# A product of zeros behind the gates, the norm factors and the last scores of a two-block network

## The chip, the cores and the metric

The kernel runs on one core of one Trainium2 chip, in one launch. Its time is the device time of that core in microseconds (us). Two runs took 2160.47 and 2160.67, a median of 2160.57.

## The reference, cut to what matters

The input is x, 256 tokens of 1024 float32 features. A first block mixes compressed, selected and windowed attention with a pooling mixer and adds a feed-forward layer (1024 to 4096 to 1024, squared ReLU). A second block has two layers: sliding-window attention, then a gated short convolution, each followed by an expert layer ("PEER") with 16384 experts:

```python
q = (xt @ w_query).reshape(T, PEER_HEADS, 2, QUERY_HALF)
s = jnp.einsum('thpd,hpnd->thpn', q, sub_keys)        # 8 heads x 2 x 128 scores
s_top, i_top = lax.top_k(s, PEER_TOPK)                # 16 of 128
...
g_s, sel = lax.top_k(cand, PEER_TOPK)                 # 16 of the sums
g = jax.nn.softmax(g_s, axis=-1)
...
a = jnp.einsum('td,thkd->thk', xc, u)                 # u: rows of expert_u
w = gc * jax.nn.gelu(a, approximate=False)
return jnp.einsum('thk,thkd->td', w, v)               # v: rows of expert_v
```

Everything is float32. The kernel computes the expert layer densely: all 16384 experts for all tokens, with a gate that is zero for those not chosen.

## The kernel before, in words

**Split products.** A float32 matrix is read from memory in units of 128 x 1024 (`Stream`). ScalarE rounds each unit to float32r (`wh`, line 73), VectorE or GpSimd takes what is left (`wl`, line 74). The activations are split in the same way (`xh`). `dense3` (line 179) makes three products for each 128 x 128 block: high by high, high by low, low by high, each with 256 columns (the tokens) moving. They add up in a PSUM tile, `mm`. In the profile all of them have the line of the helper `mm`, L177, and are told apart by their tiles: `mm<-xh,wh` twice, then `mm<-xh,wl`. A unit holds eight blocks, so 24 split products; two units make one pair of output tiles, 48.

**Other products on TensorE.** Some come between the split ones: `sums` (line 212, one column, the sums of squares of a norm), `spread` (line 223, float32 with the identity, which lays the norm factors along all partitions), the scores of the queries against the keys (`score`, line 1023, float32, four per pair of heads; each float32 product stands as two records in the trace), transposes, and the gates.

**An expert layer** (`peer`, line 1010). After the queries and scores comes the first half, `tmode(128, h, evac_u)`: the 128 units of `peer_u` pass through split products. Beside it run two generators, in an order that is written out by hand (`tc.manual_schedule()`): `topk` finds the chosen experts on VectorE, then `gate` spreads their gates over all experts. It works on 32 groups of eight tokens; for each group its inner function `spread` (line 1253) makes 16 half-precision products of one-hot rows (tiles `misc` and `lows`) into a PSUM tile `g2`, which ScalarE and VectorE multiply onto the experts' values (`apply`). So a gates' group of 16 half-precision products comes between every 48 (sometimes 72) split ones. The second half, `mix`, has products of 512 columns with `peer_v`.

**What sets the order.** Outside the manual part the scheduler of the tile framework places the instructions; inside it they stand as written. TensorE takes its instructions in order.

Of the kernel before, what the change touches and what calls it, by code (L numbers as in the profile page):

```python
# [8 lines left out]
F32 = mybir.dt.float32  # L9
F32R = mybir.dt.float32r  # L10
# [8 lines left out]
P = 128  # L19
# [90 lines left out]
def build(tc, a):  # L110
    nc = tc.nc
    V, S, PE, G = nc.vector, nc.scalar, nc.tensor, nc.gpsimd
    ctx = ExitStack()
    glob = ctx.enter_context(tc.tile_pool(name="glob", bufs=1))
# [32 lines left out]
    ident = glob.tile([P, P], F32, name="ident")  # L147
    V.memset(cols[:, NCOL:], 1.0)
    S.activation(cols[:, NCOL:], cols[:, NCOL:], AF.Square)
    W = Stream(nc, glob, plan, pooled)  # L150
    def load_x(k):
        nc.sync.dma_start(x[:, k:k + 2], a["x"][:, k:k + 2])

    load_x(0)
    nc.sync.dma_start(cols[:, :NCOL], a["cols"])
    W.load(0)
    load_x(2)
    W.load(1)
    load_x(4)
    W.load()  # L160
    load_x(6)
    W.load()
    nc.sync.dma_start(ident, a["consts"][:, :P])
# [8 lines left out]
    def col(name, i=0):  # L172
        o = COLS[name][0] + i
        return cols[:, o:o + 1]

    def mm(out, l, r, start, stop):
        PE.matmul(out, l, r, start=start, stop=stop, skip_group_check=True)  # L177
# [11 lines left out]
    def bank():  # L189
        return pmm.tile([P, 2, T], F32, name="mm")  # L190
# [32 lines left out]
    def spread(out, r, ps):  # L223

        for t in range(2):
            mm(ps[:, 0, t * P:(t + 1) * P], r[:, t:t + 1].to_broadcast([P, P]), ident, t == 0, True)
        V.tensor_copy(out, ps[:, 0])

    def norm_pair(i, xh, sq, gain):
# [5 lines left out]
    def square(i, sq):  # L235
        d = sq[:, :2] if i == 0 else sq[:, 2 + i % 4:4 + i % 4]
        S.activation(d, x[:, i:i + 2], AF.Square)
        if i:
            V.tensor_add(sq[:, :2], sq[:, :2], d)

    def tmode(nt, xh, evac, after=None, kt=KD, lag=0):
# [5 lines left out]
        for i in range(0, nt, 2):  # L247
            ps = bank()
            if i == 0 and lag:
                w = [W.get(), W.ahead(1)]  # L250
                for lo, hi in ((0, KD - lag), (KD - lag, KD)):
                    for j in range(2):
                        for k in range(lo, hi):
                            dense3(ps[:, j], w[j], k, xh, k, k == 0, j == 1 and k == KD - 1, j == 0)
                        if hi == KD and j == 0:
                            W.get()
                yield 0.33 * 2 * KD
# [41 lines left out]
    def con(name):  # L299
        o, w = CONSTS[name]  # L300
        return cst[:, o - P:o - P + w]
# [15 lines left out]
    for i in range(0, KD, 2):  # L317
        for k in (i, i + 1):
            parts(xh, k, x[:, k], col("mix", k))
        W.pump(i // 2 - 4)  # L320
    for i in range(0, KD, 2):
        square(i, sq)
    W.pump(-1)
    V.tensor_copy(identb, ident)
    V.tensor_copy(causalb, con("causal"))
    V.tensor_copy(bandb, con("band"))
# [41 lines left out]
    def fin_norm():  # L368
        ps = pa.tile([P, 2, T], F32, name="s", bufs=4)
        V.tensor_copy(rs2, token_rstd(sq, ps, small))  # L370
        spread(rstd, rs2, ps)
# [27 lines left out]
    ps = bank()  # L399
# [17 lines left out]
    ps = bank()  # L417
# [19 lines left out]
    ps = bank()  # L437
# [223 lines left out]
    for g in range(0, 4, 2):  # L661
        ps = bank()
        for j in range(2):
            dense3(ps[:, j], (h, l), g + j, ph, g + j, True, j == 1, j == 0)
        for j in range(2):
            parts(mh, g + j, ps[:, j], col("pscale", g + j))
# [42 lines left out]
    for _ in tmode(8, ah, residual(0.5, lambda k: col("mlp", k), xh, sq), lag=2):  # L709
        pass  # L710
# [21 lines left out]
    def after_ff(i):  # L732
        if i == 0:
            ps = pf.tile([P, 2, T], F32, name="s")
            r = token_rstd(sq, ps, small)
            V.tensor_mul(r, r, r)
            spread(rstd2, r, ps)
# [221 lines left out]
    for _ in tmode(4, xh, evac_q, after_qk):  # L959
        pass  # L960
    spread(rstd2, r1s[0], pa.tile([P, 2, T], F32, name="s", bufs=3))
    late_q(2)
    turn_k()
    query_scale(0)
    ps = bank()
# [41 lines left out]
    def side_bank():  # L1007
        return px.tile([P, 2, T], F32, name="g", bufs=2)

    def peer(l, xg, sq, rest):  # L1010
# [12 lines left out]
        def score(i):  # L1023
            ps = side_bank()
            q = qs[(i // 2) % 3]
            for t in range(2):
                for p in range(2):
                    mm(ps[:, t, p * P:(p + 1) * P], q[:, p, t * P:(t + 1) * P], keys[:, i + p],
                       t == 0 and p == 0, True)
            S.copy(sc4[:, i // 2].rearrange("p t h k -> p (t h k)"), ps.rearrange("p a b -> p (a b)"))  # L1030

        def evac_q(i, ps):
            if i < 6:
                S.copy(qs[i // 2], ps)
                if i == 2:
                    hm.append(token_rstd(sq, side_bank(), small))
                if i == 4:
                    spread(rstd, hm.pop(), side_bank())
                    for q in qs:
                        V.tensor_mul(q, q, bc(rstd, 2))  # L1040
            else:
                score(i - 6)
                V.tensor_mul(qs[(i // 2) % 3], ps, bc(rstd, 2))
# [14 lines left out]
        V.scalar_tensor_tensor(t, x[:, k], col("ffn2", 8 * l + k), rstd, op0=OP.mult, op1=OP.mult)  # L1058
        parts(h, k, t)
        score(10)  # L1060
        score(12)
        score(14)
        gA2 = xhp.tile([P, 16, T], F32, name="xh1")
# [162 lines left out]
        def gate():  # L1226

            m = glob.tile([P, 4096], FP16, name="misc")
            m2 = pp.tile([P, 2048], FP16, name="lows")

            def hot(v):
                return v.rearrange("p (u i t) -> p u i t", u=4, t=2)

            o2, hi, lo = ([hot(v[:, 1024 * b:1024 * b + 1024]) for b in range(2)]
                          for v in (m[:, :2048], m[:, 2048:], m2))
            it = iota2[:, None].to_broadcast([P, 4, P, 2])

            def tok(tbl, t0):
                return tbl[:, t0:t0 + 8].rearrange("p (u t) -> p u t", t=2)[:, :, None, :].to_broadcast([P, 4, P, 2])

            N = T // 8
            pend = {}

            def onehot(gr):
                t0, b = 8 * gr, gr % 2
                V.tensor_tensor(o2[b], it, tok(i2T, t0), op=OP.is_equal)
                V.tensor_tensor(hi[b], it, tok(i1T, t0), op=OP.is_equal)
                yield 1.37
                V.tensor_mul(lo[b], hi[b], tok(glT, t0))
                V.tensor_mul(hi[b], hi[b], tok(ghT, t0))  # L1250
                yield 1.37

            def spread(gr):
                b = gr % 2
                ps = px.tile([P, 8, P], F32, name="g2", bufs=2)
                for t in range(8):
                    u, v = divmod(t, 2)
                    mm(ps[:, t], o2[b][:, u, :, v], hi[b][:, u, :, v], t % 4 == 0, False)
                    mm(ps[:, t], o2[b][:, u, :, v], lo[b][:, u, :, v], False, True)
                pend[gr] = ps.rearrange("p t i -> p i t")  # L1260

            def apply(gr):
                t0, pr, n = 8 * gr, pend.pop(gr), done[0]

                tiles = [(i0, min(max(n, i0), i1), i1, d) for i0, i1, d in
                         ((0, 64, gA0), (64, 112, gA1), (112, 128, gA2))]
                for i0, j, i1, d in tiles:
                    if j < i1:
                        S.activation(d[:, j - i0:i1 - i0, t0:t0 + 8], pr[:, j:i1], AF.Copy, scale=2.0 ** -15)  # L1269
                for i0, j, i1, d in tiles:  # L1270
                    if j > i0:
                        v = d[:, :j - i0, t0:t0 + 8]
                        V.scalar_tensor_tensor(v, pr[:, i0:j], 2.0 ** -15, v, op0=OP.mult, op1=OP.mult)  # L1273
                gated[0] = t0 + 8

            for gr in range(N + 2):
                if gr >= 2:
                    apply(gr - 2)
                    yield 1.1
                if gr < N:  # L1280
                    yield from onehot(gr)
                if 1 <= gr <= N:
                    spread(gr - 1)
# [311 lines left out]
```

## Time and profile before

| | |
|---|---|
| profiled execution, its own time | 2171.65 us |
| its span, first to last instruction | 2169.9 us |
| median of the runs | 2160.57 us |
| TensorE busy with products | 2150.2 us (99%) |
| TensorE busy with weight loads | 2006.1 us (92%) |
| VectorE, ScalarE, GpSimd busy | 1558.1, 1089.1, 242.1 us |
| mean granted TensorE clock | 0.998 of full speed |

Busy times of different engines lie beside each other. Weight loads (PEld) lie beside products (PE). Products are pipelined: the length recorded for one is longer than the time until the next can start, so a busy TensorE says nothing on how fast its products follow each other; that is read from how many there are in a stretch.

### The profile page before, as it was taken

The numbers are of one execution on the slowest core, as the hardware profiler recorded it, in microseconds if no ns is written. First come the engines' busy times: TensorE is split into PE (matmuls) and PEld (weight loads), VectorE is DVE, ScalarE is ACT, GpSimd is POOL, SyncE is SP. The second block draws the span as 40 slices with busy tenths as digits, with TensorE's granted clock in tenths as the row PEclk, the third lists the DMA queues.
The fourth block names the chain that finished last, engine by engine and source line by source line (L and its number), as shares of the span: only waits on it lengthen the run. The fifth ranks groups of instructions, "written<-read, shape, count | busy, mean of one in ns | idle before, by whom it ended". The sixth has DMA issues, their size and how long they took to land.

```text
span 2169.9 us, 39654 instructions
## 1 busy us (share of the span) xinstructions
PE 2150.2 (99%) x15892; PEld 2006.1 (92%) x15892; DVE 1558.1 (72%) x2784; ACT 1089.1 (50%) x1703; POOL 242.1 (11%) x104
## 2 busy tenths in 40 slices
PE   8999999999999999999999999999999999999999
PEld 7899999989999999988888889999999999888887
DVE  7757655766898889955555567768799996555555
ACT  5555554565545444454444454544544444444453
POOL 0000000001652112100000000056221110000000
PEclk9999999999999999999999999999999999999999
DMA  6435555325555444455555555645544445555554
GB/s 204 159 123 185 186 186 190 120 88 192 179 196 184 166 156 165 158 194 193 194 194 194 194 173 188 206 171 179 193 163 160 163 157 188 193 193 194 194 193 146
DMA packets 105625, 382.69 MB, mean 176 GB/s; under 512 B 11984, under 2 KB 12384, under 8 KB 105184
## 3 DMA queue, kind: packets, MB, share of 16 engines
q1 hardware_dynamic: 105120, 378.06, 50.5%
q8 instruction: 124, 2.03, 0.4%
q0 software_dynamic: 320, 2.11, 0.3%
q14 instruction: 61, 0.50, 0.1%
HBM read 379.07 MB, written 1.05 MB: 175 GB/s over the span
## 4 chain that ended last, share of the span: by engine, by line
PE 96%; DVE 1%; ACT 1%; DMA 1%; issue 0%; SPq 0%; ACTq 0%
PE mm L177 57%; PE g L177 36%; PE s L177 2%; PE o L177 1%; DVE wl L74 1%; ACT wh L73 1%; DMA wraw<-in_w_in 0%; DMA x<-in_x 0%; PE tp L896 0%; ACT prob L533 0%; PE tp L541 0%; ACT xh L198 0%; DVE x L980 0%; DVE nm L529 0%; DVE nmx L882 0%
## 5 line engine op out<-in xcount | busy, mean ns | idle before, releaser
L177 PE MATMUL mm<-xh,wh 128*128 128x256 f32 x6240 | 1113.3, 282 | 7.9 <-ACT wh L73 6.4
L74 DVE TENSOR_TENSOR wl<-wraw,wh 128x1024 fp32r<-128x1024 f32 (+1 forms) x622 | 765.7, 1231 | 467.5 <-ACT wh L73 463.2
L73 ACT CAST wh<-wraw 128x1024 fp32r<-128x1024 f32 (+1 forms) x716 | 752.4, 1051 | 688.0 <-PE g L177 330.8
L177 PEld LDWEIGHTS mm<-xh,wh 128*128 128x128 f32 x6240 | 956.2, 189 | 10.6 <-ACT wh L73 6.8
L177 PE MATMUL mm<-xh,wl 128*128 128x256 f32 x3120 | 876.3, 281 | 2.0 <-DVE wl L74 2.0
L177 PE MATMUL g<-wh,xh 128*128 128x512 f32 x2016 | 622.6, 389 | 0.0
L177 PEld LDWEIGHTS mm<-xh,wl 128*128 128x128 f32 x3120 | 593.0, 190 | 3.4 <-DVE wl L74 2.9
L177 PEld LDWEIGHTS g<-wh,xh 128*128 128x128 f32 x2016 | 378.5, 188 | 78.4
L177 PE MATMUL g<-wl,xh 128*128 128x512 f32 x1008 | 392.2, 389 | 0.0
L74 POOL TENSOR_TENSOR wl<-wraw,wh 128x1024 fp32r<-128x1024 f32 x94 | 238.3, 2542 | 574.7 <-ACT wh L73 574.5
L177 PEld LDWEIGHTS g<-wl,xh 128*128 128x128 f32 x1008 | 189.3, 188 | 39.0
L1329 ACT ACTIVATE gA<-mm 128x512 f32<-128x512 f32 (+14 forms) x112 | 57.1, 510 | 88.9 <-PE mm L177 88.8
L1303 DVE TENSOR_TENSOR xh<-gA,xh 128x256 fp32r<-128x256 f32 x220 | 91.9, 418 | 0.0
L177 PE MATMUL mm<-mid,wh 128*128 128x256 f32 x512 | 90.5, 281 | 0.0
L1302 ACT CAST xh<-gA 128x256 fp32r<-128x256 f32 x220 | 88.7, 403 | 0.0
L1269 ACT ACTIVATE gA<-g 128x384 f32<-128x384 f32 (+22 forms) x62 | 20.1, 341 | 131.8 <-PE g L177 131.8
L177 PEld LDWEIGHTS mm<-mid,wh 128*128 128x128 f32 x512 | 78.5, 190 | 0.0
L1273 DVE SCALAR_TENSOR_TENSOR gA<-g,gA 128x512 f32<-128x512 f32 (+27 forms) x118 | 59.7, 543 | 22.8 <-ACT xh L1269 22.1
L177 PE MATMUL mm<-mid,wl 128*128 128x256 f32 x256 | 71.9, 281 | 0.0
L177 PE MATMUL g<-misc 128*128 128x128 f16 x512 | 66.5, 220 | 0.0
L177 PE MATMUL g<-lows,misc 128*128 128x128 f16 x512 | 65.7, 219 | 0.0
L1250 DVE TENSOR_TENSOR misc<-misc,row 128x1024 f16<-128x1024 f16 x64 | 60.9, 952 | 2.2
(367 smaller groups left out, 1614.1 us busy)
## 6 DMA issues: line engine op xcount, KB each, us to landing
wraw<-in_peer_u SPq DMA_DIRECT2D x256, 512.0 KB, 3.5
wraw<-in_peer_v SPq DMA_DIRECT2D x256, 512.0 KB, 3.5
wraw<-in_w_ff SPq DMA_DIRECT2D x64, 512.0 KB, 4.3
wraw<-in_w_query SPq DMA_DIRECT2D x32, 512.0 KB, 4.0
wraw<-in_w_in SPq DMA_DIRECT2D x29, 512.0 KB, 4.1
wraw<-in_w_cin SPq DMA_DIRECT2D x24, 512.0 KB, 4.3
wraw<-in_w_qkv SPq DMA_DIRECT2D x12, 512.0 KB, 3.4
wraw<-in_w SPq DMA_DIRECT2D x8, 512.0 KB, 3.5
```

Of the source, the lines that this page charges most:

```text
L73: nc.scalar.copy(h[:, s], r[:, s])
L74: (nc.gpsimd if j in self.pooled else nc.vector).tensor_sub(l[:, s], r[:, s], h[:, s].bitcast(F32))
L177: PE.matmul(out, l, r, start=start, stop=stop, skip_group_check=True)
L1250: V.tensor_mul(hi[b], hi[b], tok(ghT, t0))
L1269: S.activation(d[:, j - i0:i1 - i0, t0:t0 + 8], pr[:, j:i1], AF.Copy, scale=2.0 ** -15)
L1273: V.scalar_tensor_tensor(v, pr[:, i0:j], 2.0 ** -15, v, op0=OP.mult, op1=OP.mult)
L1302: S.copy(w[0], gA(e))
L1303: V.tensor_sub(w[1], gA(e), w[0].bitcast(F32))
L1329: S.activation(d[:, :, n:], ps[:, :, n:], AF.Gelu)
```

## The change

A tile `zero` of float32r zeros (128 x 4) is made at the start. `lead(out)` multiplies its first two columns, as weights, with its last two, as moving columns, and adds the result, zeros, to a 2 x 2 corner of a PSUM tile that has just been written. It is called in three places: at the end of the norm factors' `spread`, in `score` for the last pair of heads, and at the end of the gates' `spread`.

```diff
+    none = glob.tile([P, 4], F32, name="none")
+    V.memset(none, 0.0)
...
+    zero = glob.tile([P, 4], F32R, name="zero")
+
+    def lead(out):
+        PE.matmul(out[:2, :2], zero[:, :2], zero[:, 2:], start=False, stop=True, skip_group_check=True)
+
...
             mm(ps[:, 0, t * P:(t + 1) * P], r[:, t:t + 1].to_broadcast([P, P]), ident, t == 0, True)
+        lead(ps[:, 0])
         V.tensor_copy(out, ps[:, 0])
...
     W.pump(-1)
+    S.copy(zero, none)
...
+            if i == 14:
+                lead(ps[:, 1])
             S.copy(sc4[:, i // 2].rearrange("p t h k -> p (t h k)"), ps.rearrange("p a b -> p (a b)"))
...
                     mm(ps[:, t], o2[b][:, u, :, v], lo[b][:, u, :, v], False, True)
+                lead(ps[:, 7])
                 pend[gr] = ps.rearrange("p t i -> p i t")
```

On TensorE this adds 72 products: 6 behind norm factors, 2 behind the last scores (one in each layer), 64 behind gates' groups. VectorE gets one fill, ScalarE one copy. Every other instruction stands in the order in which it stood.

The end of the first gates' group on TensorE, before (`g` is the PSUM tile, `misc` and `lows` the one-hot rows and gates):

```order
L177 MATMUL g_8292<-misc 128x128
L177 LDWEIGHTS misc
L177 MATMUL g_8292<-lows,misc 128x128
L177 MATMUL mm<-xh_5646,wh 128x256 x2
L177 MATMUL mm<-xh_5646,wl 128x256
```

and the same place now:

```order
L185 MATMUL g_8301<-misc 128x128
L185 LDWEIGHTS misc
L185 MATMUL g_8301<-lows,misc 128x128
L182 MATMUL g_8301<-zero 2x2
L185 MATMUL mm<-xh_5653,wh 128x256 x2
L185 MATMUL mm<-xh_5653,wl 128x256
```

The lead (L182) stands between the last half-precision product and the first split product; the readers of the group's tile now wait for it, not for the half-precision product.

The last scores of the first expert layer on TensorE, before (the tile `gA` holds queries and keys) and now:

```order
L177 MATMUL mm<-xh_5477,wl 128x256
L177 MATMUL g<-gA_5643 128x128 x16
L177 MATMUL mm<-xh_5646,wh 128x256 x2
L177 MATMUL mm<-xh_5646,wl 128x256
```

```order
L185 MATMUL mm<-xh_5484,wl 128x256
L185 MATMUL g<-gA_5650 128x128 x16
L182 MATMUL g<-zero 2x2
L185 MATMUL mm<-xh_5653,wh 128x256 x2
L185 MATMUL mm<-xh_5653,wl 128x256
```

Here too the lead stands between the last float32 product and the split products of the first half, and nothing else has moved.

## Rows read from the trace of the kernel before

**Rows 1.** The page: busy time, share, instructions by engine; the chain of waits.

```profile
PE 2150.2 (99%) x15892; PEld 2006.1 (92%) x15892; DVE 1558.1 (72%) x2784; ACT 1089.1 (50%) x1703; POOL 242.1 (11%) x104
...
PE 96%; DVE 1%; ACT 1%; DMA 1%; issue 0%; SPq 0%; ACTq 0%
```

**Rows 2.** Stretches, tile mm alone: us, busy (products), clock, DMA share, GB/s.

```profile
694.36:931.50 237.14, 211.40 (x1728) 1.00 0.48 164
1581.44:1817.70 236.26, 211.33 (x1728) 1.00 0.48 165
212.74:395.10 182.36, 182.21 (x1545) 1.00 0.54 185
540.16:681.90 141.74, 141.70 (x1248) 1.00 0.56 190
1422.14:1569.40 147.26, 147.23 (x1248) 1.00 0.53 183
...
1293.40:1381.30 87.90, 87.75 (x769) 1.00 0.62 206
```

**Rows 3.** Groups by form, 550 to 670 us: count, busy us, mean ns.

```profile
L177 PE MATMUL mm<-xh,wl 128*128 128x256 f32 x353 | 97.4, 276 | 0.0
```

**Rows 4.** The same view, 1430 to 1560 us (the same work in layer 1).

```profile
L177 PE MATMUL mm<-xh,wl 128*128 128x256 f32 x369 | 103.7, 281 | 0.0
```

**Rows 5.** The same view, 700 to 908 us (gates of layer 0).

```profile
L177 PE MATMUL mm<-xh,wl 128*128 128x256 f32 x505 | 141.9, 281 | 0.0
```

**Rows 6.** The same view, 1582 to 1794 us (gates of layer 1).

```profile
L177 PE MATMUL mm<-xh,wl 128*128 128x256 f32 x520 | 146.1, 281 | 0.0
```

**Rows 7.** Timeline of TensorE at 1381 us (start, us): one-column products.

```profile
1381.22 0.50 PE L177 MATMUL g<-cols,misc 128*128 128x1 f32 x4
```

**Rows 8.** Groups by form behind them, 1381.8 to 1387.1 us.

```profile
L177 PE MATMUL mm<-xh,wl 128*128 128x256 f32 x15 | 4.2, 281 | 0.0
```

**Rows 9.** Timeline of TensorE at 1284.5 us: a stall between split products.

```profile
1284.52 0.38 PE L177 MATMUL mm<-xh,wh 128*128 128x256 f32 x1 [0.48 <-DVE xh L199]
1284.74 0.28 PE L177 MATMUL mm<-xh,wl 128*128 128x256 f32 x1
```

**Rows 10.** Groups by form behind this stall, 1284.6 to 1289.0 us.

```profile
L177 PE MATMUL mm<-xh,wl 128*128 128x256 f32 x12 | 3.3, 276 | 0.0
```

**Rows 11.** Groups by form behind the last stall, 1375.2 to 1380.8 us.

```profile
L177 PE MATMUL mm<-xh,wl 128*128 128x256 f32 x18 | 5.0, 276 | 0.0
```

**Rows 12.** Timeline of ScalarE, 0 to 7 us.

```profile
4.40 0.63 ACT L237 ACTIVATE misc<-x 128x512 f32<-128x512 f32 x1 [2.16 <-DMA x<-in_x]
```

**Rows 13.** Timeline of TensorE, 694.2 to 695.2 us: the end of a gates' group.

```profile
694.28 0.22 PE L177 MATMUL g<-misc 128*128 128x128 f16 x1
694.34 0.22 PE L177 MATMUL g<-lows,misc 128*128 128x128 f16 x1
694.37 0.48 PE L177 MATMUL mm<-xh,wh 128*128 128x256 f32 x2
694.69 0.28 PE L177 MATMUL mm<-xh,wl 128*128 128x256 f32 x1
```

**Rows 14.** Timeline of the weight loads in the same stretch.

```profile
694.34 0.30 PEld L177 LDWEIGHTS mm<-xh,wh 128*128 128x128 f32 x2
694.57 0.19 PEld L177 LDWEIGHTS mm<-xh,wl 128*128 128x128 f32 x1
```

**Rows 15.** Groups by form of the weight loads, 0 to 100 us: 24 columns.

```profile
L177 PEld LDWEIGHTS mm<-xh,gh 128*24 128x24 f32 x24 | 2.4, 101 | 0.9 <-issue 0.3 <-PE mm L177 0.2
```

**Rows 16.** Timeline of TensorE, 539.79 to 541.0 us: the end of layer 0's scores.

```profile
539.79 0.61 PE L177 MATMUL g<-gA 128*128 128x128 f32 x4
540.16 0.48 PE L177 MATMUL mm<-xh,wh 128*128 128x256 f32 x2
540.48 0.28 PE L177 MATMUL mm<-xh,wl 128*128 128x256 f32 x1
```

**Rows 17.** A stretch, all engines' busy time: gates of layer 0.

```profile
694.50:908.00 213.50, 213.50 (x2037) 212.21 (x2036) 198.19 (x258) 98.26 (x192) 42.38 (x16) 1.00 0.47 161
```

## The prediction

> **What bounds the kernel now.** I read the page first. TensorE is busy for 2150.2 of 2169.9 us and the chain that ended last is 96% TensorE [rows 1], so a nanosecond more or less per product, on some thousands of products, is time of the whole program. VectorE is the next busiest at 72% [rows 1]. The profiled execution took 2171.65 us, the median of the runs is 2160.57: I work out the change in the profiled execution and take the sum off the median, 11 us lower.
>
> Then I read the same work in different places. The stretches' view counts the products that write the tile `mm` (the split products, 256 columns each). The expert layer's score search runs beside 1248 of them in both layers: 141.74 us in layer 0, 147.26 us in layer 1 [rows 2]. TensorE was not waiting in either (141.70 and 147.23 us busy), and the granted clock is 1.00 in both, the 2.4 GHz level. So there are **two paces**: 141.74 / 1248 = 113.6 ns a product and 147.26 / 1248 = 118.0 ns, 4.4 ns apart. The mean recorded length of one product tells them apart: 276 ns in the fast stretch [rows 3], 281 in the slow one [rows 4]. With that key the page can be walked through: the feed-forward run of 1545 products is slow (182.36 / 1545 = 118.0) [rows 2], and so is every run behind a gates' group, in layer 0 [rows 5] and layer 1 [rows 6].
>
> A pace holds until the stream of these products is broken; what breaks it seems to choose the next one. I sorted the runs by what stands ahead of them:
> - behind a gates' half-precision group: all 64 runs slow [rows 5, 6];
> - behind full-width float32 products (norm factors, scores): 12 fast and 3 slow, the long stretches of 1545 and 1248 among the three [rows 2];
> - behind products of one or two columns: 6 slow, 1 fast, the last of the seven in [rows 7, 8];
> - behind a stall of more than 0.04 us with no product of another kind in it, from the time the clock is up: 8 of 8 fast, at once or after a few products (the first run begins at 62.1 us, the last at 1374.4), two in [rows 9 to 11].
>
> **The change, part by part.** It adds 72 products of zeros ("leads"): 64 behind the gates' groups, 6 behind the spread norm factors, 2 behind the last scores. Nothing else moves on any engine. The small VectorE fill and ScalarE copy of the zeros come in the first 5 us; ScalarE idles 2.16 us before the first x lands [rows 12], which hides them: nothing.
>
> *Price of a lead behind a gates' group.* The last half-precision product starts at 694.34, 0.06 behind the one before it; the weight load of the next big product starts at 694.34 too [rows 13, 14]. Two loads take 0.30 us and one 0.19, so a load needs 0.11 before the next can start [rows 14]. The third big product starts 0.35 after the last half-precision one [rows 13]; at 0.12 each that puts the real begin of the first at 0.11, when its load is through. With the lead, the load that runs beside the last half-precision product is the lead's (a load of 24 columns is recorded with 101 ns [rows 15] against the 190 of 128, 0.86 ns a column, so two columns cost next to nothing), the lead begins at 0.06, and the big product's load starts only then: begin at 0.06 + 0.11 = 0.17, 0.06 later. 64 x 0.06 = **3.8 us**.
>
> *Price of a lead behind float32 products.* There four records take 0.61 us from 539.79; the first big product is recorded at 540.16 and the third at 540.48 [rows 16], so at the same 0.12 each it really begins at 540.24, 0.11 behind the last record, at 540.13 (the last lasts some 0.28). That record covers the load. With a lead in between, the whole load of 0.11 lies open: 8 x 0.11 = **0.9 us**.
>
> *Settling.* Some runs behind a stall need a product or two to reach the pace; I add 0.004 us each, **0.3 us**, a guess of the size of one slow product's surplus. Sum of the prices: 5.0 us. The bounds: nothing at all, if the big load slips past the lead; and 0.11 more for each of the 72, 12.9 in all, if the lead's load takes as long as a full one.
>
> *What it may give back.* With a lead, the product that follows another type is the zero product, and the big run starts behind a product of its own type with its load open for 0.11 us. In the trace that resembles the stalls inside a run, 8 of 8 fast: at 1284.52 the second product starts 0.22 after the first (0.11 of load, 0.11 of product) and the run goes on at 276 ns [rows 9, 10]. So I take the fast pace behind every lead. Slow products that would turn fast: gates 2 x 1728, less two at the head of each of 64 runs, 3328; feed-forward 1545; layer 1's search 1248 [rows 2]. Times 4.42 ns: 14.7 + 6.8 + 5.5 = **27.0 us**. The runs of 1248 in layer 0 and of 769 in layer 1 are fast already (87.90 / 769 = 114.3 [rows 2]) and stay so. VectorE could take it back: it is busy for 198.19 of 213.50 us among layer 0's gates, 93% [rows 17]. Shortened by the net 5.5 us of a layer the stretch would have it at 95%; I take nothing off.
>
> Net: 27.0 - 5.0 = 22.0 us, **2138.6 us**; with the bounds of the lead's price 2133.6 to 2146.5.
>
> A rule speaks against the price. The Trainium skill, "TensorE: Matmul & The Clock Gate", section "Step-by-step: what each phase is for", says that TensorE's queue pulls weight loads ahead of products in flight. By that the big load could run beside the last half-precision product, lead or not, the prices would be nil and the sum 2133.6. The rows show loads starting with the product just before them and none two products ahead [rows 13, 14]; I go by the rows. The same page's section "Back-to-back issue gap" gives columns / 2.4 + 2.5 ns, by which I estimate 109.2 for 256 columns: one pace, and below both that the rows show [rows 2]. By that rule alone there is no second pace to win, and only the prices would be left.
>
> **The rivals.**
> 1. *The pace stays slow and the leads are only paid for.* The lead is a narrow product, and behind narrow products 6 of 7 runs are slow [rows 7, 8]; the trace has no narrow product of the big ones' own type, so it can't say whether width or type decides. It decides at the second big product: if that starts 0.118 or less behind the real begin of the first, with nothing slipping, the run stays slow. Then 2160.57 + 5.0 = 2165.6; if the runs that are fast now behind the same places (1248, 769 and two of 48 products) turn slow too, 2113 x 4.42 ns = 9.3 more, 2174.9. Slower than before. Chance 0.27.
> 2. *It works at one kind of place.* Half-precision and float32 places differ now, and may still. Gates alone fast, the rest slow: 2160.57 + 5.0 - 14.7 + 9.3 = 2160.2, or 2150.9 where those that are fast now stay so; the long stretches alone: 2160.57 + 5.0 - 12.3 = 2153.3. Chance 0.18.
> 3. *The leads do nothing to the order of loads*, the big load running past them: without the price and with the pace 2133.6, without either 2160.6. Nothing in the rows shows a load two products ahead. Chance 0.05.
>
> **How the numbers follow.** Forecast 0.50, rivals 0.27, 0.18 and 0.05. The predicted time is the forecast's, 2138.6; its own range is 2133.6 to 2146.5. For 8 in 10 the range has to take in rival 2 (to 2160.2) and the cheaper half of rival 1: **2133 to 2168**. Left out are the dearer half of rival 1 (0.13) and the edge of the forecast (0.03). A measurement of this kernel tells about 2% from no change, 43 us. The whole gain on offer is 27 us and the worst case 14 us, so within 2% has 0.97, faster by more 0.02, slower by more 0.01.
>
> **What would show it.** In the profile of the changed kernel: (a) the mean length of the split products behind the gates' groups, 276 if the pace turned, 281 if not; (b) the stretches of 1545 and 1248 products at 175.5 and 141.7 us, or unchanged; (c) a load of the lead beside the last half-precision product, the next big load starting with the lead, and the third big product some 0.40 us behind the last half-precision one where it is 0.35; (d) the layer 0 search still at 141.7. The prediction is wrong if (a) shows 281: then its step from stalls to leads fails, and if (c) shows a longer gap, the price was mis-sized.

## The result, and the profile after

The changed kernel takes 2184.67 us (two executions, 2183.87 and 2185.47) where the kernel before took 2160.57. The ratio on record is 1.0105, 95% interval 1.0081 to 1.0129 (the ratios here and below are an estimate of their own and not the quotient of the medians, which is 1.0112 here). I had forecast 2138.6 with a range of 2133 to 2168, so the prediction is wrong, in its sign too. Measured again with more executions (the last experiments), the ratio is 1.0072 (1.0044 to 1.0100): a real loss, of the order of 1%.

The profiled execution took 2185.47 us, 13.8 more than the profiled one of before (2171.65). The page of the profile, busy times and the chain by engine, answers to [rows 1]:

```profile
span 2183.7 us, 39800 instructions
...
PE 2164.8 (99%) x15964; PEld 2020.3 (93%) x15964; DVE 1558.3 (71%) x2785; ACT 1087.9 (50%) x1704; POOL 239.2 (11%) x104
...
PE 97%; DVE 1%; ACT 1%; DMA 0%; issue 0%; SPq 0%; ACTq 0%
```

TensorE has its 72 products more and is busy 14.6 us longer, about the whole loss; VectorE, ScalarE and GpSimd are within 3 us of before, none of them more than 0.2 us longer. The stretches of [rows 2], tile `mm` alone (start:end, us, busy and count of TensorE, clock, DMA share, GB/s); the windows of the gates end with the last product here, so the two of before are given once more with that end. Before, then the short runs of layer 0 (48 products each) from the norm factors to the last scores:

```profile
694.36:929.10 234.74, 211.16 (x1728) 1.00 0.48 164
1581.44:1815.35 233.91, 211.09 (x1728) 1.00 0.48 165
505.70:540.16 34.46, 28.50 (x240) 1.00 0.47 169
```

After:

```profile
700.00:936.10 236.10, 211.13 (x1728) 1.00 0.49 163
1593.01:1829.10 236.09, 211.11 (x1728) 1.00 0.48 163
211.80:394.20 182.40, 182.21 (x1545) 1.00 0.55 185
540.64:687.90 147.26, 147.23 (x1248) 1.00 0.54 183
1433.65:1581.00 147.35, 147.23 (x1248) 1.00 0.55 182
1300.62:1391.50 90.88, 90.88 (x769) 1.00 0.60 197
505.07:540.64 35.57, 29.50 (x240) 1.00 0.50 164
```

The gates pay 1.4 and 2.2 us for their leads and gain nothing. Of the four long runs of products the two that were slow stay slow, and the two that were fast turn slow: 141.74 to 147.26 us (5.5) and 87.90 to 90.88 (3.0). That is 12.0 of the 13.8 us. The five short runs between the norm factors and the last scores turn slow as well, 34.46 to 35.57 us, and the same five in layer 1 (34.47 to 35.57), though only the first of each five has a lead ahead of it: 2.2 us more. Together these make 14.2; the rest of the program is some 0.4 us shorter. The clock is 1.00 throughout, so this is no matter of its level. The mean length of a split product behind the leads, 700 to 914 us of layer 0 and 1593 to 1806 of layer 1, is still 281 ns as in [rows 5, 6]:

```profile
L185 PE MATMUL mm<-xh,wl 128*128 128x256 f32 x519 | 145.8, 281 | 0.0
...
L185 PE MATMUL mm<-xh,wl 128*128 128x256 f32 x516 | 145.0, 281 | 0.0
```

The end of a gates' group, TensorE's timeline (start, us) beside [rows 13]:

```profile
699.92 0.22 PE L185 MATMUL g<-lows,misc 128*128 128x128 f16 x1
699.94 0.20 PE L182 MATMUL g<-zero 128*2 128x2 f32 x1
700.00 0.48 PE L185 MATMUL mm<-xh,wh 128*128 128x256 f32 x2
700.32 0.28 PE L185 MATMUL mm<-xh,wl 128*128 128x256 f32 x1
```

And the weight loads there, beside [rows 14]:

```profile
699.92 0.08 PEld L182 LDWEIGHTS g<-zero 128*2 128x2 f32 x1
699.98 0.30 PEld L185 LDWEIGHTS mm<-xh,wh 128*128 128x128 f32 x2
```

The lead's own load stands beside the last half-precision product, the next big load 0.06 us behind it, and the third big product comes 0.40 us after the last half-precision one, 0.35 before: the price went as worked out.

### The profile page after: what moved, and what is told of

Read it like the earlier page. It is cut to its first block, busy times and chain, and to the rows that moved or that the text cites. A ratio compares the mean times of both kernels' runs of the same rounds, so it can differ in the third digit from the quotient of the medians.

```text
span 2183.7 us, 39800 instructions
## 1 busy us (share of the span) xinstructions
PE 2164.8 (99%) x15964; PEld 2020.3 (93%) x15964; DVE 1558.3 (71%) x2785; ACT 1087.9 (50%) x1704; POOL 239.2 (11%) x104
## 4 chain that ended last, share of the span: by engine, by line
PE 97%; DVE 1%; ACT 1%; DMA 0%; issue 0%; SPq 0%; ACTq 0%
PE mm L185 58%; PE g L185 35%; PE s L185 1%; PE o L185 1%; ACT wh L73 0%; DVE wl L74 0%; DMA x<-in_x 0%; PE tp L906 0%; DMA wraw<-in_w_in 0%; ACT prob L543 0%; PE tp L551 0%; DVE x L990 0%; ACT xh L206 0%; DVE nm L539 0%; DVE nmx L892 0%
## 5 line engine op out<-in xcount | busy, mean ns | idle before, releaser
L1339 ACT ACTIVATE act<-mm 128x512 f32<-128x512 f32 (+30 forms) x74 | 30.1, 407 | 65.8 <-PE mm L185 28.1
```

What stands on the lines that cost most here:

```text
L1339: S.activation(t[:, :, :n], ps[:, :, :n], AF.Gelu)
```

## Experiments

**1. The kernel before, again, and the change in pieces.** The prediction took the paces of one profiled execution for a property of the kernel. Four kernels on one chip, with the kernel before beside them (30 executions, median 2163.33, 2155.54 to 2172.30).

*No edit: the kernel before.*

> The kernel before once more, unchanged. Its timed runs (2160.5, 2160.7) were 11 us under its own profiled execution (2171.65). Theory P (a run of split products keeps the pace that it starts with, and a start can go either way): the times of this kernel fall into groups some 5 to 7 us apart, as the 1545-product run (6.9 us) or the 1248-product run (5.5 us) is fast or slow, and the profile shows at which pace each long run went in its own execution; if the profiled execution takes near 2160, at least one of the two is fast in it. Theory Q (profiling itself costs the 11 us): every profiled execution stands at 2171 to 2172 with both long runs slow and all timed ones at 2160.5.

Measured: 2161.57 us (2155.11 to 2167.59), ratio 0.9992 (0.9969 to 1.0015). Its profiled execution took 2155.49, 16 us less than the other one of the same code, so it is not the profiling that costs 11 us. The stretches (tile `mm`, columns as above) of the long runs and of layer 0's gates:

```profile
211.60:387.00 175.40, 175.36 (x1545) 1.00 0.55 191
530.67:672.40 141.73, 141.71 (x1248) 1.00 0.56 190
1411.53:1553.40 141.87, 141.70 (x1248) 1.00 0.56 190
684.44:918.35 233.91, 211.09 (x1728) 1.00 0.48 164
```

The runs of 1545 and of layer 1's 1248 products, slow in [rows 2], are fast here, in the same program. **The pace of the same run behind float32 products differs from one execution to the next**; behind a gates' half-precision group it does not (62 of 62 runs are slow in either profile, leaving out the last of each layer, in whose tail other products mix). Behind a stall it differs too. Near 182 us this trace has one at the place where the trace of before has one at 184; TensorE's timeline (the second row starts 0.27 us after the first, where some 0.11 is usual):

```profile
182.04 0.28 PE L177 MATMUL mm<-xh,wl 128*128 128x256 f32 x1
182.31 0.38 PE L177 MATMUL mm<-xh,wh 128*128 128x256 f32 x1
182.53 0.28 PE L177 MATMUL mm<-xh,wl 128*128 128x256 f32 x1
```

Groups by form ahead of it (178 to 181.9 us) and behind it (183 to 187), count, busy us and mean ns:

```profile
L177 PE MATMUL mm<-xh,wl 128*128 128x256 f32 x11 | 3.0, 276 | 0.0
...
L177 PE MATMUL mm<-xh,wl 128*128 128x256 f32 x12 | 3.4, 281 | 0.0
```

From 276 to 281: here the run is slow behind the stall. In the trace of before the run goes on at 276 behind the same stall. In three of the profiles below (the first sweep, the changed kernel again, and 2x64 at the float32 places alone) the run turns from 276 to 281 at this place as well. The "8 of 8" of the prediction were eight draws of one execution.

*Leads at the gates alone:*

```
-        lead(ps[:, 0])
...
-            if i == 14:
-                lead(ps[:, 1])
```

> Leads behind the 64 gates' groups alone. Theory P (a lead makes the run behind it slow): those runs were slow before, so only the price of the leads is left, 64 x 0.04 to 0.06 us, 2.8 to 3.8 us over before; the 1248-product run of layer 0 and the 769-product run stay fast. Theory R (each added product costs the same, 24 us / 72 = 0.33): plus 21 us. Theory L (the moved tiles cost it): plus most of 24 us, and the same in the run with the tiles alone.

Measured: 2162.31 us (2160.63 to 2171.76), ratio 1.0000 (0.9981 to 1.0018). In its profile all 62 gates' runs are slow, as without leads. The expectation that layer 0's run of 1248 stays fast missed: with no lead ahead of it, it takes 147.30 us here, and the run of 1545 is fast (175.41). The 3.5 us that the leads cost in the profile after lie inside this interval (up to 1.0018, 3.9 us).

*Leads at the spread norm factors and last scores alone:*

```
-                lead(ps[:, 7])
```

> Leads behind the six spread norm factors and the two last scores alone. Theory P: these eight turn long runs slow, so nearly all of the loss comes from here: plus 11 us against the profiled execution of before, 18 to 22 us against its timed runs. Theory R: 8 x 0.33, plus 2.7 us. Theory L: as in the run with the tiles alone.

Measured: 2180.05 us (2163.55 to 2182.64), ratio 1.0069 (1.0041 to 1.0096). The eight leads at float32 places carry nearly the whole loss, though not in every execution: one of the nine took 2163.55, the median of before. The long runs of its profile:

```profile
212.64:395.05 182.41, 182.21 (x1545) 1.00 0.55 185
539.89:687.20 147.31, 147.24 (x1248) 1.00 0.54 183
1297.65:1388.60 90.95, 90.84 (x769) 1.00 0.60 198
1430.47:1577.80 147.33, 147.23 (x1248) 1.00 0.53 183
```

*The tile of zeros and its fill, no lead at all:*

```
-        lead(ps[:, 0])
...
-                lead(ps[:, 1])
...
-                lead(ps[:, 7])
```

> No leads; the two small tiles, the fill and the copy stay, so that every later tile in SBUF lies where the changed kernel has it. Theories P and R: within the spread of before, whatever that is (2160 to 2172). Theory L: plus 10 us or more over every run of before.

Measured: 2164.68 us (2156.22 to 2179.67), ratio 1.0006 (0.9980 to 1.0032): the tile and its fill cost nothing that can be measured. Three of its ten executions lie above the 2172.30 that was the most of the 30 beside it. The profiled one was the worst, 2179.67 us, with all four long runs slow and not one lead: nearly the whole price of the change can come by chance, without it.

**2. Does the width decide, or the type, or the open load?** The theory that the moment at which a run starts, to some nanoseconds, sets its pace, against a theory of the open weight load (any product of the runs' own type with a small load should do alike) and one of the change of type. Leads at the gates alone, a different shape at each of 16 groups in turn:

```
+LEADS = [[(2, 2)], [(2, 16)], [(2, 32)], [(2, 64)], [(2, 96)], [(2, 128)], ...]
...
+    def lead(out, m=2, n=2):
+        PE.matmul(out[:m, :n], zero[:, :m], zero[:, :n], start=False, stop=True, skip_group_check=True)
...
+                for m, n in LEADS[gr % 16]:
+                    lead(ps[:, 4:].rearrange("p t i -> p (t i)"), m, n)
```

*Two weight columns, 2 to 512 moving columns:*

> Leads behind the gates' groups alone, always two columns of weights, with 2, 16, 32, 64, 96, 128, 160, 192, 224, 240, 256, 264, 272, 288, 320 and 512 columns moving, one width for each group in turn, so that each width stands four times in the trace. What is read is the pace behind each (276 or 281 ns) and the start of the third big product behind the last half-precision one (0.35 us without a lead, some 0.40 with 2 x 2). Theory W (a short lead leaves the big product's load open, and a run that begins with an open load goes slow; the load needs 0.11 us): slow up to about 240 columns, fast from 256 on, where the lead lasts as long as the load. Theory T (whatever follows a half-precision group in float32r starts a slow run): slow at all sixteen. Theory O (the starting offset decides, in steps of a few ns): slow and fast change back and forth with the width, at each width the same in all four places.

Measured: 2163.47 us (the kernel before beside it 2167.60, one execution each, which says nothing between draws). The groups by form tell: behind 2x32 (707.1 to 712 us), 2x64 (713.9 to 718.6), 2x128 (729.6 to 734.6), 2x160 (736.3 to 741) and 2x512 (801.3 to 806):

```profile
L186 PE MATMUL mm<-xh,wl 128*128 128x256 f32 x15 | 4.2, 281 | 0.0
...
L186 PE MATMUL mm<-xh,wl 128*128 128x256 f32 x15 | 4.1, 276 | 0.0
...
L186 PE MATMUL mm<-xh,wl 128*128 128x256 f32 x15 | 4.2, 281 | 0.0
...
L186 PE MATMUL mm<-xh,wl 128*128 128x256 f32 x15 | 4.1, 276 | 0.0
...
L186 PE MATMUL mm<-xh,wl 128*128 128x256 f32 x14 | 3.9, 281 | 0.0
```

Each shape gave the same pace in all four of its places. Fast: 64, 96, 160, 256, 272, 288 and 320 columns; slow: 2, 16, 32, 128, 192, 224, 240, 264 and 512. That is no threshold in width, all of them have the same small load, and all are of the runs' own type: both rivals fall. What is left, by exclusion and not shown by a row, is the moment at which the run starts, which a lead of another width moves.

*Other weight columns, two or four leads, none:*

```
+LEADS = [[(30, 2)], [(64, 2)], [(96, 2)], [(128, 2)], ..., [(2, 2), (2, 2)], ..., []]
```

> Leads behind the gates' groups alone, shapes (weight columns x moving columns) in turn: 30x2, 64x2, 96x2, 128x2, 30x128, 64x128, 128x128, 30x256, 64x256, 96x256, 128x256, 128x512, two of 2x2, four of 2x2, two of 2x256, and none. Theory W: slow wherever the lead moves 2 or 128 columns, fast with 256 and 512 whatever the weights. Theory T: slow at all. Theory O: a mixture without order in width. Price, by theory P of the load: 128 weight columns cost 0.11 us more than 2, each further 2x2 lead some 0.03 to 0.06.

Measured: 2168.72 us (before 2167.60). Slow behind 30x2, 96x2, 128x2, 30x128, 64x128, 128x128, 128x512, four 2x2, two 2x256 and none; fast behind 30x256, 64x256, 96x256, 128x256 and two 2x2; behind 64x2 two of four fast. Two leads of 2x2 do what one does not: groups by form behind two (779.2 to 783.8 us) and four (785.8 to 790.5):

```profile
L186 PE MATMUL mm<-xh,wl 128*128 128x256 f32 x14 | 3.9, 276 | 0.0
...
L186 PE MATMUL mm<-xh,wl 128*128 128x256 f32 x14 | 3.9, 281 | 0.0
```

**3. The shape that works.** Three kernels on one chip, beside the kernel before (17 executions, median 2162.26).

*2x64 at the gates alone:*

```
-                lead(ps[:, 7])
+                lead(ps[:, 7], 2, 64)
```

> Leads behind the gates' groups alone, 2 weight columns x 64 moving columns in place of 2 x 2. Theory O (the offset at which the run starts decides, and in the sweep 2 x 64 gave the fast pace in 4 places of 4): about 3300 products of the gates' runs go at 113.3 ns in place of 117.8, 14.7 us gained, 64 x 0.05 us paid, net 11 us under before; the runs without a lead keep drawing as before, so the times spread over some 15 us around 2152. Theory T (float32r behind half precision is slow, the sweep's fast runs a chance of their neighbours): 3 us over before.

Measured: 2148.35 us (2143.56 to 2162.62), ratio 0.9942 (0.9923 to 0.9961). That is some 12.5 us, where 11 had been expected. All 62 gates' runs turn fast: the 1728 products of layer 0's gates take 228.36 us instead of 234.74, the lead's price paid:

```profile
691.24:919.60 228.36, 203.60 (x1728) 1.00 0.50 168
```

*2x64 at all three kinds of places:*

```
+        lead(ps[:, 0], 2, 64)
...
+                lead(ps[:, 1], 2, 64)
...
+                lead(ps[:, 7], 2, 64)
```

> The same leads of 2 x 64 in all three kinds of places. Theory O says nothing of which pace they give behind float32 products, where the lead starts at another offset, but it has to be one pace at each place, in nearly all executions: with the long runs all fast 2145 to 2148 and a small spread, with all of them slow 2170 to 2173. Theory D (behind float32 products each execution draws anew, lead or not): a spread of 10 us and more, as without leads there.

Measured: **2145.65 us** (2144.09 to 2149.73), ratio 0.9928 (0.9906 to 0.9950): the best version, better than both kernels, and its six executions lie within 6 us of each other. In the three kernels with wider leads at the float32 places the scheduler also puts some products of layer 0's attention in another order; that stretch takes 68.20 us here (395.35 to 463.55) and 68.19 before (404.14 to 472.33), so it is no part of the gain. Layer 0's gates, then the long runs:

```profile
683.89:912.20 228.31, 203.55 (x1728) 1.00 0.50 168
210.48:386.00 175.52, 175.36 (x1545) 1.00 0.56 191
530.05:671.80 141.75, 141.72 (x1248) 1.00 0.56 190
1405.70:1547.40 141.70, 141.69 (x1248) 1.00 0.57 189
```

The same place as above, the end of a gates' group:

```profile
683.81 0.22 PE L185 MATMUL g<-lows,misc 128*128 128x128 f16 x1
683.84 0.22 PE L182 MATMUL g<-zero 128*2 128x64 f32 x1
683.89 0.47 PE L185 MATMUL mm<-xh,wh 128*128 128x256 f32 x2
684.21 0.28 PE L185 MATMUL mm<-xh,wl 128*128 128x256 f32 x1
```

The third big product stands 0.40 us behind the last half-precision one, as with 2x2. The price is the same; only the pace that follows differs (276 ns, 684 to 893 us):

```profile
L185 PE MATMUL mm<-xh,wl 128*128 128x256 f32 x523 | 144.3, 276 | 0.0
```

*2x64 at the gates, 64x256 at the float32 places:*

```
+        lead(ps[:, 0], 64, 256)
...
+                lead(ps[:, 1], 64, 256)
```

> 2 x 64 behind the gates' groups, 64 x 256 behind norm factors and last scores: a lead that streams for as long as a load takes, fast in 4 places of 4 behind half precision. Theory W (with the load covered, the run starts fast): the runs of 1545, 1248, 769 and 1248 products at 276 ns in the profile, 2145 to 2149 with a spread of few us. Theory O: one pace at each place, either one. Theory D: spread as without leads.

Measured: 2146.66 us (2144.53 to 2152.69), ratio 0.9929 (0.9905 to 0.9952), the same as the last within the intervals. In its profile three of the four long runs are fast, the one of 769 slow (90.84 us), which misses the expectation of theory W, four fast.

**4. More executions.** Two kernels on one chip, beside the kernel before (16 executions, median 2163.97).

*No edit: the changed kernel.*

> The changed kernel once more, for more executions of it. Theory (a 2x2 zero product ahead of a run sets the slow pace, everywhere and every time): every execution between 2181 and 2187, median 2184, a spread of under 5 us where the kernel before spreads over 16; all four long runs (1545, 1248, 769 and 1248 products) at 118.0 ns in the profiled execution. Rival (its two timed executions were two bad draws): executions spread from about 2165 to 2185, median near 2175.

Measured: 2176.48 us (2172.97 to 2187.30, seven executions), ratio 1.0072 (1.0044 to 1.0100). My theory misses here: it is not every time. In the profiled execution the runs of 1545 and 769 products (710 of them before a stall) are fast behind a 2x2 lead, the two of 1248 slow:

```profile
211.61:387.20 175.59, 175.35 (x1545) 1.00 0.57 192
531.98:679.30 147.32, 147.23 (x1248) 1.00 0.54 183
1291.98:1372.80 80.82, 80.79 (x710) 1.00 0.59 197
1421.15:1568.50 147.35, 147.23 (x1248) 1.00 0.55 183
```

So behind float32 products the 2x2 lead does not fix the pace, it makes the slow pace likelier; and 2184.67 us were two dear draws.

*2x64 at the float32 places alone:*

```
-                lead(ps[:, 7], 2, 64)
```

> Zero products of 2x64 behind the spread norm factors and the last scores alone, none behind the gates' groups. Theory (2x64 sets the fast pace also behind float32 products): the long runs at 113.6 ns and the gates at 118.0 in the profiled execution, the time near the best draws of the kernel before, median 2156, every execution from 2154 to 2161. Rival (2x64 only acts behind half-precision products, and the good figure of the kernel with all leads at 2x64 was six good draws): median 2163, spread over 2156 to 2172 as before.

Measured: 2158.30 us (2155.36 to 2162.33), ratio 0.9977 (0.9960 to 0.9995): close to the theory's 2156, and clear of before, though two executions (2161.72 and 2162.33) lie above the 2161 expected as the most. The gates stay slow, the long runs are fast:

```profile
213.09:389.20 176.11, 175.46 (x1546) 1.00 0.57 192
532.65:674.60 141.95, 141.75 (x1249) 1.00 0.56 190
1413.98:1557.00 143.02, 142.82 (x1257) 1.00 0.56 189
```

Over all profiles, the four long runs in each (1545, 1248, 769 and 1248 products), counted by what stands directly ahead of them:

| ahead of the long runs | profiles | fast pace | slow pace |
|---|---|---|---|
| float32 products, no lead | 7 | 16 | 12 |
| a 2x2 lead | 3 | 2 | 10 |
| a 2x64 lead | 2 | 8 | 0 |
| a 64x256 lead | 1 | 3 | 1 |

These are not all draws of their own. In each layer a run of 48 follows the norm factors, and four more runs of 48 follow one group of float32 scores each. In all 13 profiles, both layers, those four have the pace of the first (104 of 104); the run of 1248 behind the last scores keeps it in 11 of 14 cases without a lead. So scores mostly hand a pace on, and what stands directly ahead of a run is not all that counts. The first run is fast in 13 of 14 cases without a lead, in 1 of 6 behind 2x2, 4 of 4 behind 2x64 and 2 of 2 behind 64x256: a lead at the norm factors also decides over runs that have no lead ahead of them.

## Why the prediction was wrong

**Two paces: right.** 113.6 and 118.0 ns a product come back (175.40 / 1545 = 113.5, 182.40 / 1545 = 118.1). The estimate of 109.2 ns by the Trainium skill, "TensorE: Matmul & The Clock Gate", section "Back-to-back issue gap", is met by no long run; the section gives its formula for isolated products, not for a stream with a weight load to each. The shortest stretch of 1248 products, 141.70 us with 2x64 at all places, makes 113.5.

**The price: right.** Forecast 3.8 us for 64 leads; the gates' stretches grew by 1.36 and 2.18, 3.5 together. The 0.11 at float32 places holds too: from the first of the four float32 records to the third big product 0.78 us before (212.28 to 213.06) and 0.89 after (211.23 to 212.12). The 0.3 for settling was a guess that no run singles out. The Trainium skill, "TensorE: Matmul & The Clock Gate", section "Step-by-step: what each phase is for", has the queue pull weight loads ahead of products in flight, which, taken so far that the big load passes the lead, would make the price nil. The loads' rows after show it starting 0.06 us behind the lead's load, so here it does not pass.

**From stalls to leads: the step that failed.** "So I take the fast pace behind every lead", 27.0 us of the sum, brought nothing at the gates and a loss elsewhere. Two things were wrong in it. The eight stalls were eight cases of one execution, and the stall near 182 us of another showed the slow pace. And the resemblance (open load, own type) is not what sets the pace: leads alike in both gave either pace, by their width. A lead of 2x2 happens to be one that leads to the slow pace, behind half-precision products always (62 of 62 in three profiles), behind float32 products mostly (10 of 12).

**The mix of one profile taken for the kernel's: wrong as well.** The sum went off the median with the paces of the profiled execution, 11 us slower than the median. The kernel before lies anywhere between 2155 and 2173 us by its draws, so its two timed executions will have had more of the long runs at the fast pace than its profile shows, and the leads will have taken more from them than the 9.3 us of the runs that the trace had as fast. This is argued: they have no trace of their own.

**Rival 1 named the outcome, not the reason**, at its dearer end: "if the runs that are fast now behind the same places turn slow too", 5.0 + 9.3 = 14.3 us over its base. Profile against profile it is 13.8; how close that comes is in part luck, since in the second profile of the changed kernel two of the four long runs are fast. Its reason, that a narrow product ahead leaves the run slow, fell with the sweeps: 2x64 gives the fast pace and 128x512 the slow one. Against the medians it is 24.1 (2184.67 - 2160.57); the other 10, by the same argument as above, are the draw of the two timed executions of before against that of its profile. I gave this rival 0.27 and left its dearer half outside the range; with three of the 15 runs behind full-width products slow in the trace, a draw was there to be suspected, the more as eight of those 15 stand behind scores and only kept the pace of the run ahead.

**Rival 2** describes what the shape 2x64 does not do: it works at both kinds of places (62 of 62 and 8 of 8). **Rival 3** fell with the loads' rows. The within-2% chance of 0.97 held.

What remains open: that the start's moment, to some nanoseconds, is the cause is what the sweeps leave over, and no experiment moved that moment alone. The kept traces bear it out in one kind of place. Behind scores without a lead, over all 13 profiles, the second split product starts 205 to 207 ns after the first in the 90 runs that go fast and 200 or 201 ns in the 28 that go slow. The difference is there before the pace is, but it is no rule for other places: behind 2x64 at the gates the runs start with 199 or 200 ns and go fast. Why one 2x64 lead gives the fast pace and one 2x2 does not, no run here tells.

## What to carry to other kernels

When one trace shows the same instructions at two paces, profile the unchanged kernel a second time before building on what seems to select them: eight cases of eight in one execution did not hold in the next, and the two executions were 16 us apart. If a pace is chosen where a stream restarts, sweep the shape of what restarts it in one kernel (16 shapes at 64 places took one execution): 2x2 lost 0.7 to 1% and 2x64, at the same price, won 0.7%. A kernel whose executions spread over 16 us has something undecided in it; here what decides it also narrowed the spread, to 6 us over six executions.

## What was not expected of the hardware

- A run of 256-column products keeps one of two paces, 113.5 or 118.1 ns, for up to 1545 products at a granted clock of 1.00, and the same code takes the one or the other in different executions (the run of 1545 in 182.36 and in 175.40 us).
- A product of zeros of 2x64 directly ahead turned all 62 gates' runs fast; 2x32 and 2x128, in four places each, left the run slow. One 2x2 lead leaves it slow, two of them turn the run fast, four do not. A group of float32 scores between two runs of 48 products leaves the pace as it was, 104 of 104 times.
- A lead of 64 columns costs what one of 2 columns costs: 0.40 us from the last half-precision product to the third big one, in both.
